# A transformer trunk on one core: loading x feature-major in the first stage and taking its norm sums, and the first scale columns, from single-column matmuls

## The chip, the cores and the metric

The kernel runs on one core of one Trainium2 chip. A core has TensorE (PE in the profile: matmuls, with the weight loads as PEld), VectorE (DVE), ScalarE (ACT), GpSimd (POOL) and SyncE (SP, which here issues nearly all DMA loads). The metric is device microseconds of one execution, the lower the better. The runs shown are medians over three executions.

## The reference, cut to what matters

The network has two layers, 512 tokens of 1024 features, all in float32. Before each mixer and each FFN the input is normed and then scaled and shifted by vectors that come from a condition vector c:

```python
def rms_norm(x, g):
    y = xf * lax.rsqrt(jnp.mean(xf * xf, axis=-1, keepdims=True) + EPS)
    return (y * g.astype(jnp.float32)).astype(x.dtype)

def ada_modulation(c, w, b):
    m = jax.nn.silu(c) @ w + b
    shift, scale, gate = jnp.split(m, 3, axis=-1)

h = rms_norm(x, mix_pre_g[i]) * (1.0 + scale) + shift
qkv = (h @ w_qkv)
```

So the first products need, for each token, one factor (1 over the root of the mean square of its 1024 features) and, for each feature, one scale and one shift, each a sum over 1024 products of silu(c) with a column of the modulation weight. After this first stage come the stick-breaking attention, its output projection, a SwiGLU FFN, a gMLP mixer and a second FFN; the change does not touch them.

## The kernel before

**Operands.** Every float32 product is made from high and low parts: a high part is a copy rounded to the matmul's reduced type (fp32r) by ScalarE, a low part is the difference, by VectorE (`split`, and `wemit` for weights: names wh and wl, made from raw). One product of a tile is three matmuls (`mm3`): high by high, high by low, low by high. The names hTh and hTl are the parts of h, feature-major (features on partitions): eight tiles, here called columns 0 to 7, of 128 features by 512 tokens.

**First stage.** x is loaded token-major in four tiles of 128 tokens by 1024 features. For each, `norm0` squares and sums the rows on ScalarE (accum_out), takes root and reciprocal, and VectorE multiplies the rows by the factor; here the factor is a scalar per partition. `turn0` transposes each tile on TensorE (eight transposes, name tp), and ScalarE or VectorE copies the result out of PSUM into the feature-major tiles xhT.

**Scale columns.** For columns 0 and 1, `row0` makes a row of 256 sums on TensorE (silu(c), name sc, is the stationary column, the weight block of 128x256 moves through; result ab in one partition), VectorE copies the row, and two small matmuls turn it into columns. `scales` adds the biases and multiplies by the norm weights. For columns 2 to 7 the weights are loaded in pairs of columns (blocks of 128x2x512, name ada from ada0p, four blocks for a pair): VectorE sums them in `ada0_sum` (eight operations of 128x512, name acc), and `sums0` closes the sum over the partitions with four single-column matmuls. `h0` makes column k of h: two ScalarE operations with scale and shift (hTh, and the same unrounded, in place) and one VectorE subtraction (hTl).

**Order.** `v_step` and `qk0_step` multiply column k by the weights of v (first half of its features) and of the first pair of heads (pq, pk). The code issues column by column; a loop over three pairs follows columns 0 and 1. Within this stage the order on each engine is chosen by the framework's scheduler from the order in the code and the dependencies, not by hand. From the second half of v on (`pe["chain"] = True` ahead of it) the order of TensorE is the written one, and in the attention VectorE's too. The calls `order` and the flags `chain` of the helper classes at L64 to L99 write such an order.

**Loads.** SyncE issues loads in the order of the code. Weights pass through two buffers named raw (`wload`); a third load waits until VectorE has read the first. The modulation blocks of this stage have eight buffers (tag ra). Loads for columns 2 to 7 stand behind the weight loads in the same queue:

```python
    wqk0.append(wget(("wqk", 0, 1), 0))
    wload()
    acc = ada0_sum(a2, 512, 2)
```

G in the trace is the sum for the gate vector of the first mixer, which VectorE does in the background (`Bg`, bg0).

Of the kernel before, what the change touches and what calls it, by code (L numbers as in the profile page):

```python
# [13 lines left out]
P = 128  # L14
T = 512
# [18 lines left out]
def trunk(ctx: ExitStack, tc: tile.TileContext, A: dict, out: bass.AP):  # L34
# [21 lines left out]
    def slot(dt, name, a=2, b=512):  # L56
        return s4.tile([P, a, b], dt, tag="s4", name=nm(name))
# [302 lines left out]
    x0, a0 = [], []  # L360
    for tt in range(NT):
        xt = slot(F32, "x0", 1, 1024)
        load(xt[:, 0, :], A["x"][tt * P : (tt + 1) * P, :])
        x0.append(xt[:, 0, :])
        if tt == 0:
            identt = consts.tile([P, P], F32, name="identt")
            load(identt[:], A["consts"][:, 0, :])
            cols = consts.tile([P, 4, KD], F32, name="cols")
            load(cols[:], A["cols"])
        elif tt == 3:  # L370
            a0.extend(ada0_raw(0, q) for q in range(2))
    wload()
# [303 lines left out]
    xhT = [slot(F32, "xhT") for _ in range(4)]  # L676

    def norm0(tt):
        xt = x0[tt]
        junk = npool.tile([P, D], F32, tag="n", name=nm("junk"))  # L680
        sx = small.tile([P, 1], F32, tag="sx", name=nm("sx"))
        act.activation(junk[:], xt, AF.Square, accum_out=sx[:])
        sd, r1 = rms(sx[:])
        dve.reciprocal(r1[:], sd[:])
        dve.tensor_scalar(xt, xt, r1[:, 0:1], None, ALU.mult)

    def turn0(tt):
        xt = x0[tt]
        for q in range(2):
            ps = bank("tp0")  # L690
            for k in range(4):
                kk = q * 4 + k
                transpose(ps[:, k * P : (k + 1) * P], xt[:, kk * P : (kk + 1) * P])
            for k2 in range(2):
                dst = xhT[q * 2 + k2][:, :, tt * P : (tt + 1) * P]
                src = ps[:, k2 * 256 : (k2 + 1) * 256].rearrange("p (a b) -> p a b", a=2)
                if q and tt < 2:
                    dve.tensor_copy(dst, src)
                else:
                    act.activation(dst, src, AF.Copy)  # L700
# [37 lines left out]
    onec = oneb[:, 0:1]  # L738

# [24 lines left out]
    def row0(raws):  # L764

        ps = bank("ab0", "p")
        for q, raw in enumerate(raws):
            for k in range(4):
                mm(ps[0:1, :256], sc[:, q * 4 + k : q * 4 + k + 1], raw[:, k, :], q + k == 0, q * 4 + k == 7)
        row = stp.tile([P, 256], F32, tag="row", bufs=2, name=nm("row"))  # L770
        dve.tensor_copy(row[0:1, :], ps[0:1, :256])
        ps = bank("ab0", "p")
        for i in range(2):
            mm(ps[:, i : i + 1], row[0:1, i * P : (i + 1) * P], oneb[0:1, 0:1], True, True)
        return ps

    def scales(ps, k):

        ab = small.tile([P, 2, 2], F32, tag="ab", name=nm("ab"))
        dve.tensor_tensor(ab[:, 0, :], ps[:, :2], add[:, k, :], ALU.add)  # L780
        dve.tensor_tensor(ab[:, 0, :], ab[:, 0, :], mul[:, k, :], ALU.mult)
        return ab

    def h0(ab, i, k):

        xk = xhT[k // 2][:, k % 2, :]
        h, l = hTk(hT, k, 0, T)
        for out in (h, xk):
            act.activation(out, xk, AF.Identity, scale=ab[:, i, 0:1], bias=ab[:, i, 1:2])
        dve.tensor_tensor(l, xk, h.bitcast(F32), ALU.subtract)  # L790
# [8 lines left out]
    norm0(0)  # L799
    norm0(1)  # L800
    turn0(0)
    norm0(2)
    ab0 = row0(a0)
    turn0(1)
    norm0(3)
    turn0(2)
    turn0(3)
# [869 lines left out]
```

## Time and profile before

| What | Value |
|---|---|
| Runs, us | 1104.66, 1107.62, 1107.95; median 1107.62 |
| Profiled execution: span, us | 1104.6 (first to last instruction; the page lists no other time of its own) |
| Instructions | 18512 |
| PE / PEld busy | 98% / 89% |
| DVE / ACT / POOL busy | 86% / 54% / 3% |
| Mean granted TensorE clock | 0.998 |
| HBM read / written | 164.69 MB / 8.39 MB |

Times in the text are microseconds from the first instruction of the profiled execution. A row of a timeline has the start, the duration of the group, the engine, the line, the operation, the tile written, the tiles read, the shapes and the count; in square brackets stands how long the engine was idle before it, and what ended that. A matmul's duration holds its pipeline, so two starts tell more than one duration. A busy share of 98% therefore does not say that TensorE is at its peak.

### The profile page before, as it was taken

The page shows a single profiled execution, that of the slowest core. Times are in us where ns is not written, and L with a number is a line of the kernel's source. Part 1 is how long each engine was busy: PE and PEld are TensorE (multiplying, and loading weights), DVE is VectorE, ACT ScalarE, POOL GpSimd, SP SyncE. Part 2 cuts the span into 40 slices and gives each one's busy share as a digit, 9 for nine tenths or more (in the row PEclk, how much of TensorE's full clock was granted, in tenths as well). Part 3 has the DMA queues.
Part 4 walks back from the last instruction along what each step waited for, and adds up shares of the span by engine and source line. Part 5 has one row for each costly group of instructions (what it writes and reads, how often), then busy time and mean ns, then how long its engine had stood idle before and what let it go on. Part 6 is the DMA issues. An engine that isn't in the chain of part 4 may idle for free.

```text
span 1104.6 us, 18512 instructions
## 1 busy us (share of the span) xinstructions
PE 1085.9 (98%) x7404; PEld 979.0 (89%) x7404; DVE 945.9 (86%) x1248; ACT 594.2 (54%) x982; POOL 29.5 (3%) x53
## 2 busy tenths in 40 slices
PE   6999999999999999999999999999999999999997
PEld 4787788788999999998888889988999999989996
DVE  4988999966989999989866967668979999899997
ACT  6554665665655555554243626426555555565662
POOL 0020100000000000000000000001000000000000
PEclk9999999999999999999999999999999999999999
DMA  8976434304433434359757465334334343333252
GB/s 302 370 226 217 142 116 133 125 11 152 157 112 131 162 119 146 132 197 351 272 191 256 144 205 196 96 116 155 128 117 155 128 159 102 110 115 96 77 187 81
DMA packets 51355, 176.38 MB, mean 160 GB/s; under 512 B 6074, under 2 KB 9146, under 8 KB 51268
## 3 DMA queue, kind: packets, MB, share of 16 engines
q1 hardware_dynamic: 48708, 166.81, 44.6%
q0 software_dynamic: 2560, 8.39, 2.1%
q8 instruction: 58, 0.95, 0.3%
q14 instruction: 29, 0.24, 0.1%
HBM read 164.69 MB, written 8.39 MB: 157 GB/s over the span
## 4 chain that ended last, share of the span: by engine, by line
PE 90%; DVE 4%; DMA 2%; ACT 2%; issue 1%; SPq 0%; DVEq 0%; ACTq 0%
PE r L109 32%; PE y L109 18%; PE pqk L109 7%; PE gu L109 6%; PE v L109 5%; PE X L109 4%; PE u L109 4%; PE Y L109 3%; PE av L109 2%; PE z L109 2%; PE tw L117 1%; PE tp L117 1%; PE Z L109 1%; PE W L109 1%; PE ab L109 1%
## 5 line engine op out<-in xcount | busy, mean ns | idle before, releaser
L87 ACT ACTIVATE wh<-raw 128x1024 fp32r<-128x1024 f32 (+1 forms) x112 | 115.7, 1038 | 130.5 <-PE y L109 39.4
L109 PE MATMUL r<-Sh,wh 128*128 128x256 f32 x608 | 168.1, 276 | 0.5 <-ACT e L87 0.5
L109 PE MATMUL r<-Sh,wl 128*128 128x256 f32 x608 | 167.9, 276 | 0.0
L109 PE MATMUL r<-Sl,wh 128*128 128x256 f32 x608 | 167.9, 276 | 0.0
L109 PE MATMUL y<-wh,as 128*128 128x512 f32 x480 | 149.9, 390 | 0.0
L178 DVE TENSOR_TENSOR wl<-raw,wh 128x1024 fp32r<-128x1024 f32 x87 | 105.8, 1222 | 48.2 <-ACT wh L87 47.6
L109 PEld LDWEIGHTS r<-Sh,wh 128*128 128x128 f32 x608 | 114.1, 188 | 1.0 <-ACT e L87 0.9
L109 PEld LDWEIGHTS r<-Sl,wh 128*128 128x128 f32 x608 | 114.1, 188 | 0.1
L109 PEld LDWEIGHTS r<-Sh,wl 128*128 128x128 f32 x608 | 114.1, 188 | 0.0
L109 PEld LDWEIGHTS y<-wh,as 128*128 128x128 f32 x480 | 90.0, 188 | 18.6
L71 DVE TENSOR_TENSOR wl<-f,wh 128x1024 fp32r<-128x1024 f32 x87 | 103.2, 1220 | 0.0
L87 ACT ACTIVATE wh<-f 128x1024 fp32r<-128x1024 f32 x87 | 91.8, 1055 | 15.3 <-DVE f L71 11.6
L87 ACT ACTIVATE e<-r 128x256 f32<-128x256 f32 x114 | 43.7, 385 | 101.8 <-PE r L109 100.8
L109 PE MATMUL y<-wl,as 128*128 128x512 f32 x240 | 93.7, 391 | 0.0
L109 PE MATMUL r<-hTh,wh 128*128 128x256 f32 x304 | 84.2, 277 | 0.2 <-DVE gu L71 0.2
L109 PE MATMUL r<-hTl,wh 128*128 128x256 f32 x304 | 84.0, 276 | 0.0
L109 PE MATMUL r<-hTh,wl 128*128 128x256 f32 x304 | 84.0, 276 | 0.0
L109 PE MATMUL r<-hTh,b 128*128 128x256 f32 x304 | 57.9, 276 | 0.0
L109 PEld LDWEIGHTS r<-hTh,wh 128*128 128x128 f32 x304 | 57.1, 188 | 0.9 <-DVE gu L71 0.9
L109 PEld LDWEIGHTS r<-hTh,wl 128*128 128x128 f32 x304 | 57.1, 188 | 0.0
L109 PEld LDWEIGHTS r<-hTl,wh 128*128 128x128 f32 x304 | 57.1, 188 | 0.0
L87 ACT ACTIVATE wh<-rawx 128x1024 fp32r<-128x1024 f32 x38 | 40.4, 1063 | 29.8 <-PE r L109 29.0
(262 smaller groups left out, 2937.1 us busy)
## 6 DMA issues: line engine op xcount, KB each, us to landing
rawada<-in_ada SPq DMA_DIRECT2D x80, 512.0 KB, 5.7
rawy<-in_wy SPq DMA_DIRECT2D x38, 512.0 KB, 4.6
rawx<-in_wx SPq DMA_DIRECT2D x38, 512.0 KB, 3.7
raw<-in_wdown SPq DMA_DIRECT2D x22, 512.0 KB, 5.4
raw<-in_wdn SPq DMA_DIRECT2D x22, 512.0 KB, 3.6
raw<-in_wqk SPq DMA_DIRECT2D x16, 512.0 KB, 3.9
ada<-in_ada0p SPq DMA_DIRECT2D x12, 512.0 KB, 6.3
raw<-in_wgu SPq DMA_DIRECT2D x12, 512.0 KB, 3.5
```

The lines of the kernel that those rows point to most:

```text
L71: b = getattr(nc.vector, op)(*args, **kw)
L87: b = nc.scalar.activation(*args, **kw)
L109: b = nc.tensor.matmul(o, l, r, start=start, stop=stop, skip_group_check=True)
L117: last_tp[0] = nc.tensor.transpose(o, i, ident)
L178: last_low[0] = nc.vector.tensor_tensor(l[:], raw[:], h[:].bitcast(F32), ALU.subtract)
```

## The change

The host lays x out feature-major a second time (xT: four tiles of 128 features by 2 by 512 tokens); the first stage reads that one. The first three quarters are loaded whole, the last in two halves; the two blocks for scale column 0 (a0) are loaded after the second and after the fourth quarter, and the first weight (v) in two halves. The other loads keep their order.

The norm sums come from squares: ScalarE squares each quarter (sq), VectorE adds the squares up to one tile of 128x512 and leaves the last half for itself, and TensorE sums over the partitions with single-column matmuls (the squares are the stationary operand, a column of ones moves; result st, one column for 128 tokens). Root and reciprocal are made for all 512 tokens at once. The factors lie across partitions then, so they are spread: VectorE scales the identity by each column of factors (dg), and four matmuls with a stationary tile of ones give rb, the factors of 512 tokens in each partition. `scaled0` multiplies a column of x by rb (columns 0 and 1) or by its copy rs (columns 2 to 7) on VectorE, in place. `h0` is as before, cut in two functions.

For columns 0 and 1, `sums1` takes the place of `row0` and `scales`: the weight block is the stationary operand, a column of sc moves, 16 single-column matmuls for a column, and the biases are put in by a matmul with the identity.

From the first `sums1` to column 1 the order on TensorE, ScalarE and VectorE is written out by the chain flags. In it the first weight's high parts stand ahead of column 0's activations, its low parts around hTl of column 0, and the parts of the first qk weight behind column 1's activations.

```diff
-    for tt in range(NT):
-        xt = slot(F32, "x0", 1, 1024)
-        load(xt[:, 0, :], A["x"][tt * P : (tt + 1) * P, :])
...
+    for j, cuts in enumerate((1, 1, 1, 2)):
+        for i in range(cuts):
+            c = slice(2 * i // cuts, 2 * (i + 1) // cuts)
+            load(xT[j][:, c, :], A["xT"][j][:, c, :])
...
+        elif j == 1:
+            a0.append(ada0_raw(0, 0))
+        elif j == 3:
+            a0.append(ada0_raw(0, 1))
...
+    def squares0():
+
+        for j in range(3):
+            act.activation(sq[j][:], xT[j][:], AF.Square)
+            if j:
+                dve.tensor_tensor(sq[0][:], sq[0][:], sq[j][:], ALU.add)
+        dve.tensor_tensor(sq[0][:, 0, :], sq[0][:, 0, :], sq[0][:, 1, :], ALU.add)
+        for i in range(2):
+            act.activation(sq[3][:, i, :], xT[3][:, i, :], AF.Square)
+        dve.tensor_tensor(sq[0][:, 0, :], sq[0][:, 0, :], sq[3][:, 0, :], ALU.add)
+
+    def stats0():
+
+        mm(st[:, 0:NT], ident, zero[:], True, False)
+        for i, s in enumerate((sq[0][:, 0, :], sq[3][:, 1, :])):
+            for tt in range(NT):
+                mm(
+                    st[:, tt : tt + 1], s[:, tt * P : (tt + 1) * P], onec,
+                    False, i == 1 and tt == NT - 1,
+                )
+        sd = small.tile([P, NT], F32, tag="sd0", bufs=1, name=nm("sd"))
+        last_sqrt[0] = act.activation(sd[:], st[:, 0:NT], AF.Sqrt, bias=epsb[:], scale=1.0 / D)
+        r = small.tile([P, NT], F32, tag="r0", bufs=1, name=nm("r"))
+        dve.reciprocal(r[:], sd[:])
+        for tt in range(NT):
+            dve.tensor_scalar(dg[:, tt, :], ident, r[:, tt : tt + 1], None, ALU.mult)
+            mm(rb[:, tt * P : (tt + 1) * P], onef[:], dg[:, tt, :], True, True)
+
+    def scaled0(k, rb):
+        xk = xT[k // 2][:, k % 2, :]
+        dve.tensor_tensor(xk, xk, rb, ALU.mult)
...
+    def sums1(ps, raw, k, q):
+
+        if q == 0:
+            mm(ps[:, 0:2], ident, add[:, k, :], True, False)
+        for kk in range(4):
+            for i in range(2):
+                mm(
+                    ps[:, i : i + 1], raw[:, kk, i * P : (i + 1) * P],
+                    sc[:, q * 4 + kk : q * 4 + kk + 1], False, q * 8 + kk * 2 + i == 15,
+                )
...
+    pe["chain"] = act.chain = dve.chain = True
+    sums1(pa[0], a0[0], 0, 0)
+    squares0()
+    stats0()
+    for i in range(2):
+        act.activation(wvh[:, i, :], rawv[:, i, :], AF.Copy)
+    ab0 = sums1(pa[0], a0[1], 0, 1)
+    scaled0(0, rb[:])
+    a2 = [ada0_raw(2, q) for q in range(4)]
+    high0(ab0, 0, 0)
+    scaled0(1, rb[:])
+    sums1(pa[1], a1[0], 1, 0)
+    for i in range(2):
+        dve.tensor_tensor(wvl[:, i, :], rawv[:, i, :], wvh[:, i, :].bitcast(F32), ALU.subtract)
+        if i == 0:
+            low0(0)
...
+    act.activation(rs[:], rb[:], AF.Copy)
...
+    ab1 = sums1(pa[1], a1[1], 1, 1)
+    high0(ab1, 0, 1)
+    wqk0.append(wget(("wqk", 0, 0), 0))
+    low0(1)
+    pe["chain"] = act.chain = dve.chain = False
     wqk0.append(wget(("wqk", 0, 1), 0))
     wload()
     acc = ada0_sum(a2, 512, 2)
     for b in range(1, 4):

+        for k in (2 * b, 2 * b + 1):
+            scaled0(k, rs[:])
         ps = cols0(2 * b)
```

104 lines of the change are left out of this document (38 added, 66 removed).

## The prediction

> **What bounds the kernel now.** I read the page's first part, then busy time by stretches, then the timelines of the engines in the first 75 us, because the change ends there.
>
> ```profile
> span 1104.6 us, 18512 instructions
> PE 1085.9 (98%) x7404; PEld 979.0 (89%) x7404; DVE 945.9 (86%) x1248; ACT 594.2 (54%) x982; POOL 29.5 (3%) x53
> ```
>
> TensorE is busy 98% of the span, so time can only come from a stretch in which it does no useful work, and a delay put into a dense stretch stays. The stretches of the first stage (columns: busy us and count of PE, PEld, DVE, ACT, POOL, then granted clock, DMA share, GB/s):
>
> ```profile
> 0.00:7.84 7.84, 0.00 (x1) 0.00 (x1) 1.29 (x9) 4.22 (x6) 1.19 (x6) 1.00 0.67 207
> 7.84:23.72 15.88, 15.04 (x69) 8.18 (x69) 6.58 (x16) 12.18 (x26) 0.00 (x0) 1.00 0.97 398
> 25.16:52.02 26.86, 26.27 (x128) 20.98 (x128) 25.57 (x39) 11.42 (x14) 1.42 (x2) 1.00 0.94 356
> ```
>
> Until 23.72 TensorE transposes x and makes two rows of sums; none of that is a product of the layer. From 25.16 to 52.02 two engines are full at once: PE 26.27 and DVE 25.57 of 26.86 us. The rows of VectorE and ScalarE that frame this stretch:
>
> ```profile
> 21.00 0.85 ACT L87 ACTIVATE hTh<-xhT,ab 128x512 fp32r<-128x512 f32 x1
> 25.16 0.73 DVE L71 SCALAR_TENSOR_TENSOR acc<-ada,sc,acc 128x512 f32<-128x512 f32 x1
> 26.39 0.16 DVE L71 TENSOR_TENSOR ab<-ab,add 128x2 f32<-128x2 f32 x1 [0.51 <-PE ab L109]
> 43.39 0.16 DVE L71 TENSOR_TENSOR ab<-ab,mul 128x4 f32<-128x4 f32 x1
> 46.51 1.29 DVE L71 TENSOR_TENSOR hTl<-xhT,hTh 128x512 fp32r<-128x512 f32 x2
> 52.02 0.16 DVE L71 TENSOR_TENSOR ab<-ab,mul 128x4 f32<-128x4 f32 x1
> 52.21 1.53 ACT L87 ACTIVATE hTh<-xhT,ab 128x512 fp32r<-128x512 f32 x2 [4.74 <-DVE ab L71]
> ```
>
> and of TensorE:
>
> ```profile
> 7.84 1.97 PE L117 MATMUL tp<-identt,x 128*128 128x128 f32 x8 [7.84 <-DVE x L71]
> 12.55 5.12 PE L109 MATMUL ab<-ada,sc 128*1 128x256 f32 x16
> 18.82 1.42 PE L117 MATMUL tp<-identt,x 128*128 128x128 f32 x11
> 20.17 3.61 PE L109 MATMUL ab<-ada,sc 128*1 128x256 f32 x16
> 23.72 0.50 PE L109 MATMUL v<-wh,hTh 128*128 128x512 f32 x1
> 42.41 0.95 PE L109 MATMUL ab<-oneb,acc 128*128 128x1 f32 x8
> 43.22 0.48 PE L109 MATMUL pk<-hTh,wh 128*128 128x512 f32 x1
> 44.46 0.50 PE L109 MATMUL v<-wh,hTh 128*128 128x512 f32 x1 [0.31 <-ACT hTh L87]
> 54.25 0.39 PE L109 MATMUL v<-wh,hTh 128*128 128x512 f32 x1
> ```
>
> Columns 2 to 7 of the layer's input h need scale columns (ab), which VectorE sums up in acc. At 44.46 TensorE waits 0.31 us for hTh of column 4: here VectorE's list sets the pace. For columns 6 and 7 it ends at 52.02; the first of the two hTh is there near 52.98 (52.21 and half of 1.53), and TensorE takes it at 54.25. So VectorE has 1.27 us of cover at the last pair and none at the pair before. This is what decides: a change that lengthens VectorE's list up to the row at 52.02 by more than it starts that list earlier makes TensorE wait.
>
> **The change part by part.** Prices come from groups of rows with their shapes kept apart (count | busy us, mean ns), first 60 us:
>
> ```profile
> L71 DVE SCALAR_TENSOR_TENSOR acc<-ada,sc,acc 128x512 f32<-128x512 f32 x24 | 18.0, 749 | 0.6
> L178 DVE TENSOR_TENSOR wl<-raw,wh 128x1024 fp32r<-128x1024 f32 x7 | 8.5, 1218 | 0.3 <-ACT wh L87 0.3
> L71 DVE TENSOR_TENSOR hTl<-xhT,hTh 128x512 fp32r<-128x512 f32 x8 | 5.2, 684 | 3.2 <-ACT xhT L87 3.2
> L71 DVE TENSOR_SCALAR x<-x,r 128x1024 f32<-128x1024 f32 x4 | 3.0, 754 | 0.1
> L71 DVE RECIPROCAL r<-sd 128x1 f32<-128x1 f32 x4 | 0.6, 160 | 2.0 <-ACT sd L87 1.9
> L87 ACT ACTIVATE junk<-x 128x1024 f32<-128x1024 f32 x4 | 4.2, 1050 | 2.7 <-DMA x<-in_x 2.7
> L87 ACT ACTIVATE vf<-v 128x512 f32<-128x512 f32 x2 | 1.2, 598 | 3.0 <-PE v L109 2.9
> L87 ACT ACTIVATE sd<-sx,epsb 128x1 f32<-128x1 f32 x4 | 1.2, 295 | 0.1
> ```
>
> Loads: SyncE's rows:
>
> ```profile
> 8.12 0.33 SPq L126 DMA_DIRECT2D raw<-in_wqk  x1
> 9.37 0.33 SPq L126 DMA_DIRECT2D ada<-in_ada0p  x1
> 10.64 0.33 SPq L126 DMA_DIRECT2D ada<-in_ada0p  x1
> 11.87 0.33 SPq L126 DMA_DIRECT2D ada<-in_ada0p  x1
> 24.93 0.33 SPq L126 DMA_DIRECT2D raw<-in_wv  x1
> 25.36 2.11 SPq L126 DMA_DIRECT2D ada<-in_ada0p  x4
> ```
>
> Each of the four issues from 8.12 on comes when the load eight places before it has landed (x1, x2, x3, the first scale block), so 512 KB land every 1.25 us. The bytes stay the same and the rate is the limit; only the order moves. A scale block now stands between the second and the third quarter of x, so I put the second quarter at 8.1, the scale block at 9.35, the third at 10.6, the last halves at 11.2 and 11.85, the second scale block at 13.1. The last of x comes 1.25 later than now. The two extra issues (halves) cost nothing while loads stand ahead of them.
>
> Norm: Squares on ScalarE: 1.05 each, halves 0.60 by the vf row, done at 12.9. VectorE adds: two of 1.22 and two of about 0.65, the last done near 14.2. On TensorE a single-column product was there 8 times in the 0.81 us between 42.41 and 43.22, so 0.10 an instruction, two instructions a matmul. The eight matmuls behind the adds take 1.6, to about 16.0. Then square root 0.30, reciprocal 0.16, four scalings of 128x128 (between 0.16 and 0.754; I take 0.2, nearest to the small row), and the last spread matmul (0.25, from 11 transposes in the 1.35 us from 18.82 to 20.17): 17.8. What is removed (32 transposes, their 16 evacuations, four scalings of x by rows at 0.754) lay before 21.0, so none of it shortens VectorE's later list. The copy of the spread factors out of PSUM (0.60) runs on ScalarE behind column 0's activations, while ScalarE waits for the next ab; without that cover the multiplies from column 2 on would start 0.6 later. The memsets of ones and zeros run on engines that wait for the loads.
>
> First scale columns: Sixteen instructions of 0.10 and the product behind them: 19.6. They replace row products of 5.12 and 3.61, which needed a row copy and a turn as well. Then the first multiply by the spread factors, 0.65: hTh starts at 20.4 against 21.00, so 0.6 earlier, and TensorE's first product at 21.2 against 23.72, since the second row (3.61) no longer stands before it.
>
> VectorE until 52.02: With the multiply for column 1, the two low halves of the first weight and hTl of column 0 it is free for acc at about 23.4 against 25.16: -1.75. Into its list come six multiplies of full tiles, for columns 2 to 7. The hTl rows have the same kind and size: 0.684 alone, 1.29 for the two at 46.51, so 3.9 to 4.1; I take +3.9, as they come in pairs. The low half of the first qk weight now comes behind column 1's activations, so it moves into the list: +1.2. Out go the 0.51 us before 26.39, which acc can fill, and one small add: -0.65. Sum -1.75 + 3.9 + 1.2 - 0.65 = +2.7 on the row at 52.02. The cover takes 1.27 of it; TensorE reaches the end of the first products 1.4 us later. ScalarE loses work in the stretch (11.42 of 26.86 busy), which buys nothing.
>
> [...]
>
> What is late next: The second half of v:
>
> ```profile
> 66.39 2.36 DVE L178 TENSOR_TENSOR wl<-raw,wh 128x1024 fp32r<-128x1024 f32 x2 [0.45 <-ACT wh L87]
> 67.85 0.39 PE L109 MATMUL v<-wh,hTh 128*128 128x512 f32 x1
> ```
>
> The first wl is done at 66.39 + 1.18 = 67.57, and TensorE uses it at 67.85: 0.28 of cover. If VectorE carries all of 2.7 that far, TensorE loses 2.4; if its later sums give way, 1.4. I take the middle, +1.9. Against its own execution the sum is 1104.6 + 1.9 = 1106.5. That span is 0.06 under the lowest of the runs (1104.66) and 3.0 under their median (1107.62); I add the step to the median: 1109.5.
>
> **The rivals.** TensorE's head start counts, and VectorE is not the bound: Place: the row that answers 52.02. If the multiplies fall into VectorE's waits, what is left is TensorE starting at 21.2 instead of 23.72 (2.5) and its wait of 0.31 at 44.46: -2.8, so 1104.8. For it: VectorE waits 3.2 us before its hTl rows today, in the first stage. Against it: after 25.16 it has 1.3 us free in all, and acc cannot move ahead of its own loads. It decides if the last ab ends before 52.
>
> VectorE starts its list late: The order of the three engines is written out through column 1; if acc is not put into VectorE's waits for column 1 (about 2 us before ab, 1.7 behind it), its list starts nearer 27.5: +1.9 + 3.7 = +5.6, 1113.2. The same time comes if TensorE runs at half pace through sums and spread: the transposes at 7.84 took 0.25 each and those at 18.82 0.12, though the granted clock reads 1.00 in that stretch. Sums, spread and columns are 1.6 + 1.0 + 1.6 = 4.2 at full pace, so up to +4.2 more. The first scale columns run from 9.4 on, which speaks against it.
>
> [...]
>
> The weight queue holds the sums up: The four loads for the second acc block stand on SyncE behind the next v weight (24.93, then 25.36), and that waits for a buffer which the moved low half frees, now near 30. A load of this kind and the start of that block:
>
> ```profile
> DMA to landing us min/median/max: 5.5/7.1/10.2
> 34.78 1.53 DVE L71 SCALAR_TENSOR_TENSOR acc<-ada,sc,acc 128x512 f32<-128x512 f32 x2
> ```
>
> Issued at 30.4, the first lands at 36 at best, where the forecast has VectorE ready for the block from 34.5 on. Low halves and multiplies can fill the gap, or not: +0 to +2, up to 1111.5.
>
> It comes out level: Later stages give the step back, 1107.6.
>
> **How the numbers follow.** Forecast (+1.4 to +2.4) 0.40; TensorE's head start 0.20; late list 0.14; weight queue 0.12; level 0.14. The likeliest one's own range is 1107.5 to 1111.5 with the spread of the runs. Changes below 0.3% (3.3 us) can't be told from none, as the three runs lie that far apart. Faster by more than that needs all of the head start and a little more: 0.15. Slower needs the late list, or the queue on top of the forecast: 0.27. Within: 0.58. The range goes from a full head start, 1103, to the late list, 1113.5.
>
> **What would show it.** Right: hTh near 20.4, the first v product near 21.2, acc from 23 to 24, the ab row for columns 6 and 7 near 54.5, a wait of TensorE for hTh at column 4 or 6 of 1 to 3 us, VectorE without gaps between. Wrong: that ab row at 52 or before (then the head start counts); acc from 27 (late list); single-column instructions at 0.2 before 20 us (slow array); VectorE waiting for ada loads near 35 (queue). If hTh starts after 21.0, the working of the norm is wrong, whatever the total.

## The result, and the profile after

The changed kernel takes 1147.12 us (median of four runs, 1144.32 to 1147.99), the kernel before 1106.61 beside it (1104.66 to 1107.95): a ratio of 1.0362, 95% interval 1.0341 to 1.0383. The forecast was 1109.5, its range ended at 1113.5. The sign was the forecast's; of the 40.5 us it had 1.9.

The page of the kernel after, its first rows (busy us, share of the span, instructions):

```profile
span 1145.4 us, 18541 instructions
PE 1122.2 (98%) x7426; PEld 1013.5 (88%) x7426; DVE 948.7 (83%) x1251; ACT 591.4 (52%) x966; POOL 29.7 (3%) x54
```

TensorE is busy 36.3 us longer (1122.2 against 1085.9) with 22 instructions more. So most of the time doesn't go into waits: the same products take longer. Where, is read from the start of the first or last instruction of some products (views by tile; us):

| Product | before | after | later by |
|---|---|---|---|
| first v product | 23.7 | 28.4 | 4.7 |
| first z product (attention) | 73.4 | 90.9 | 17.5 |
| first r product (gMLP weights) | 315.1 | 334.3 | 19.2 |
| first u product | 632.4 | 661.0 | 28.6 |
| first X product | 981.2 | 1020.7 | 39.5 |
| last store | 1101.0 | 1141.9 | 40.9 |

Two losses, then: 17.5 us until z, in the stage that was changed, and 23.4 us behind it, in code that the change does not touch; 20.3 of these grow between the first r and the first X product.

**The first stage.** TensorE's timeline of the kernel after:

```profile
9.47 3.54 PE L109 MATMUL ab<-sc,ada 128*128 128x1 f32 x16 [3.04 <-DMA ada<-in_ada0s]
14.51 3.57 PE L109 MATMUL st<-oneb,sq 128*128 128x1 f32 x16 [1.07 <-DVE sq L71]
19.06 2.04 PE L109 MATMUL rb<-dg,onef 128*128 128x128 f32 x8 [0.98 <-DVE dg L71]
20.90 3.41 PE L109 MATMUL ab<-sc,ada 128*128 128x1 f32 x16
24.60 3.55 PE L109 MATMUL ab<-sc,ada 128*128 128x1 f32 x16
28.44 2.05 PE L109 MATMUL v<-wh,hTh 128*128 128x512 f32 x4
30.29 1.91 PE L109 MATMUL v<-wl,hTh 128*128 128x512 f32 x4
32.00 1.91 PE L109 MATMUL v<-wh,hTl 128*128 128x512 f32 x4
33.70 2.21 PE L109 MATMUL ab<-sc,ada 128*128 128x1 f32 x16
38.17 0.63 PE L109 MATMUL v<-wh,hTh 128*128 128x512 f32 x1
```

Sixteen single-column instructions take 3.4 to 3.6 us, 0.22 each, four times in a row; the prediction had 0.10, from a row at 42.41. The twelve v products from 28.44 to 33.70 come every 0.44 us where the kernel before has 0.23. The array works at half pace from the first instruction (two bias instructions at 5.84 take 0.58 us, the same kind 0.28 at 27.32 in the kernel before) to about 35 us; there the fifth group of sixteen needs only 2.21. At 38.17 it is at half pace again (starts 0.43 apart until 40.73). VectorE of the kernel after:

```profile
18.63 0.87 DVE L71 TENSOR_SCALAR dg<-identt,r 128x128 f32<-128x128 f32 x4
28.64 0.75 DVE L71 SCALAR_TENSOR_TENSOR acc<-ada,sc,acc 128x512 f32<-128x512 f32 x1
35.95 0.16 DVE L71 TENSOR_TENSOR ab<-ab,mul 128x2 f32<-128x2 f32 x1 [6.57 <-PE ab L109]
47.23 0.16 DVE L71 TENSOR_TENSOR ab<-ab,mul 128x4 f32<-128x4 f32 x1
67.14 0.16 DVE L71 TENSOR_TENSOR ab<-ab,mul 128x4 f32<-128x4 f32 x1 [1.72 <-PE ab L109]
```

It begins its list at 28.64 with one operation and then stands 6.57 us: the second column's factors come next in its order, and TensorE has them late. The row that answers 52.02, the factors of columns 6 and 7, comes at 67.14. Stretches from 36 us on (columns as in the prediction), kernel after:

```profile
36.00:40.00 4.00, 3.37 (x11) 2.67 (x12) 4.00 (x7) 3.52 (x4) 0.00 (x0) 0.74 0.00 0
44.00:48.00 4.00, 2.63 (x14) 1.94 (x14) 3.99 (x8) 1.63 (x2) 0.75 (x2) 1.00 0.98 355
48.00:52.00 4.00, 3.71 (x10) 2.94 (x11) 3.96 (x8) 3.31 (x5) 0.67 (x1) 0.57 1.02 413
60.00:64.00 4.00, 3.70 (x12) 2.92 (x13) 3.89 (x7) 4.00 (x7) 0.00 (x0) 0.72 0.34 136
```

In two places the granted clock falls in the stretch behind one in which TensorE stood (idle 1.37 of 4 us at 44, clock 0.57 at 48; idle 0.80 of 4 us at 56, clock 0.72 at 60). In the kernel before, all these stretches show 1.00. The account from the first v to the first z product, one stretch of each kernel, before first:

```profile
23.72:73.40 49.68, 49.09 (x229) 39.58 (x228) 45.45 (x57) 22.70 (x30) 9.56 (x18) 1.00 0.84 302
```

```profile
28.44:90.90 62.46, 58.45 (x237) 46.56 (x237) 46.21 (x61) 24.56 (x32) 9.58 (x18) 0.92 0.70 251
```

The stretch is 12.8 us longer. TensorE is idle 4.0 against 0.6 us: 3.4. Granted clock, 58.45 at 0.92: 4.7. Half pace from 28.44 to 35, which the granted clock doesn't show (it reads 1.00 there): 5.3 us for twelve products instead of 2.8, and 0.3 in the sums behind them: 2.8. That leaves 1.9, of which the dearer single product (next) is about 1.2 (237 at 5 ns). With the 4.7 of the later start this is the 17.5.

**The later stages.** Groups with their shapes kept apart (count | busy us, mean ns), before and after:

```profile
L109 PE MATMUL r<-Sh,wh 128*128 128x256 f32 x608 | 168.1, 276 | 0.5 <-ACT e L87 0.5
L109 PE MATMUL y<-wh,as 128*128 128x512 f32 x480 | 149.9, 390 | 0.0
```

```profile
L109 PE MATMUL r<-Sh,wh 128*128 128x256 f32 x608 | 171.1, 281 | 0.0
L109 PE MATMUL y<-wh,as 128*128 128x512 f32 x480 | 152.1, 395 | 0.0
```

Same counts, same shapes, no waits, and each product 5 ns dearer. Nothing in these rows says why; that is what the first experiments ask.

### The profile page after: what moved, and what is told of

It is laid out like the page before. It is cut to its first block, busy times and chain, and to the rows that moved or that the text cites. A ratio compares the mean times of both kernels' runs of the same rounds, so it can differ in the third digit from the quotient of the medians.

```text
span 1145.4 us, 18541 instructions
## 1 busy us (share of the span) xinstructions
PE 1122.2 (98%) x7426; PEld 1013.5 (88%) x7426; DVE 948.7 (83%) x1251; ACT 591.4 (52%) x966; POOL 29.7 (3%) x54
## 4 chain that ended last, share of the span: by engine, by line
PE 96%; DVE 2%; ACT 1%; DMA 1%; issue 0%; SPq 0%; DVEq 0%; ACTq 0%
PE r L109 33%; PE y L109 18%; PE v L109 8%; PE pqk L109 7%; PE gu L109 6%; PE X L109 4%; PE u L109 4%; PE Y L109 3%; PE av L109 2%; PE z L109 2%; PE tw L117 1%; PE Z L109 1%; PE W L109 1%; PE tp L117 1%; PE ab L109 1%; DMA xT<-in_xT 1%
## 5 line engine op out<-in xcount | busy, mean ns | idle before, releaser
L87 ACT ACTIVATE wh<-raw 128x1024 fp32r<-128x1024 f32 (+2 forms) x113 | 115.7, 1030 | 142.8 <-PE y L109 48.1
L109 PE MATMUL r<-Sh,wh 128*128 128x256 f32 x608 | 171.1, 281 | 0.0
L109 PE MATMUL r<-Sh,wl 128*128 128x256 f32 x608 | 170.7, 281 | 0.0
L109 PE MATMUL r<-Sl,wh 128*128 128x256 f32 x608 | 170.6, 281 | 0.0
```

The lines of the kernel that those rows point to most:

```text
L87: b = nc.scalar.activation(*args, **kw)
L109: b = nc.tensor.matmul(o, l, r, start=start, stop=stop, skip_group_check=True)
```

## The experiments

Eighteen kernels. Ratios are against the kernel before on the same chip (its medians there were 1105.77 to 1106.49).

| Run | Median us | Ratio, 95% interval |
|---|---|---|
| after, addresses as before (e1) | 1124.74 | 1.0175 [1.0156, 1.0194] |
| before, with the three tiles (e2) | 1129.99 | 1.0225 [1.0210, 1.0241] |
| before, slots moved by 64 bytes (e3) | 1128.39 | 1.0209 [1.0189, 1.0229] |
| before, all moved by 32 (e4) | 1105.81 | 1.0003 [0.9991, 1.0016] |
| before, slots by 128 (e12) | 1112.19 | 1.0059 [1.0043, 1.0076] |
| before, slots by 32 (e17) | 1126.80 | 1.0183 [1.0167, 1.0200] |
| before, slots by 192 (e18) | 1128.06 | 1.0191 [1.0176, 1.0206] |
| e1, array kept busy (e5) | 1124.73 | 1.0169 [1.0137, 1.0201] |
| e1, norm part alone (e6) | 1120.30 | 1.0130 [1.0114, 1.0145] |
| before, columns part alone (e7) | 1120.07 | 1.0131 [1.0112, 1.0149] |
| before, array kept busy (e8) | 1104.78 | 0.9990 [0.9981, 1.0000] |
| e5, acc into the wait (e9) | 1122.70 | 1.0146 [1.0130, 1.0162] |
| e5, no six multiplies (e10) | 1117.58 | 1.0103 [1.0088, 1.0118] |
| e5, busy in the wait (e11) | 1125.73 | 1.0174 [1.0149, 1.0199] |
| e1, busy between sums (e13) | 1120.35 | 1.0131 [1.0114, 1.0148] |
| e13, acc into the wait (e14) | 1117.91 | 1.0110 [1.0095, 1.0125] |
| e14, no six multiplies (e15) | 1118.79 | 1.0113 [1.0098, 1.0128] |
| e6, array kept busy (e16) | 1120.37 | 1.0122 [1.0107, 1.0138] |

### The later stages: three small tiles

The change adds three tiles of four floats per partition: `zero` in the pool of constants, `sd0` and `r0` in the pool of small tiles. As the author read the compiled kernel's memory plan, each takes 32 bytes per partition, the constants lie ahead of the weight tiles, and the small tiles between the weight tiles and the slots of the activations. So the weight tiles begin 32 bytes later and the slots 96 (the plan itself is not shown here; the expectations of e1 to e4 go by these figures). One run takes the displacement out of the change, three put it into the kernel before.

e1, the change with its three tiles in the first stage's own pool:

```diff
-    zero = consts.tile([P, NT], F32, name="zero")
+    zero = stp.tile([P, NT], F32, name="zero")
...
-        sd = small.tile([P, NT], F32, tag="sd0", bufs=1, name=nm("sd"))
+        sd = stp.tile([P, NT], F32, name=nm("sd"))
...
-        r = small.tile([P, NT], F32, tag="r0", bufs=1, name=nm("r"))
+        r = stp.tile([P, NT], F32, name=nm("r"))
```

> The changed kernel with its three small new tiles (zero, sd, r of the norm) moved from the long-lived pools to the pool of the first stage, so that all later tiles lie at the addresses that they have in the kernel before (in the changed kernel the weight tiles wh and wl lie 32 bytes higher, the activation slots and the FFN's work tiles 96 bytes higher). Nothing else differs. Theory addresses: the part of the loss behind the first stage (40.8 less the 17.5 by which the first z product is late, so 23) goes, time near 1124, r matmuls at 276 ns mean instead of 281, first z product still near 91. Rival (another order of instructions or the slower start carried on): 1146, r matmuls stay at 281 ns.

e2, the kernel before with three tiles that nothing reads; e3 has only the loop, e4 only `zero`:

```diff
+    zero = consts.tile([P, NT], F32, name="zero")
+    dve.memset(zero[:], 0.0)
+    for t in ("sd0", "r0"):
+        dve.memset(small.tile([P, NT], F32, tag=t, bufs=1, name=nm(t))[:], 0.0)
```

> The kernel before with three tiles of 16 bytes per partition added that nothing reads, in the pools where the change adds its own: weight tiles +32 bytes, activation slots and FFN tiles +96, as in the changed kernel. Theory addresses: 1106.6 + 23 = 1130, first z product unmoved near 73.4, r matmuls 281 ns. Rival: 1106.6.

> The kernel before with only two of these tiles: weight tiles at their old addresses, activation slots and all that follows +64 bytes. If the distance between the stationary and the moving operand counts (64 bytes changed, as in the changed kernel): 1130. If the place of the weights alone counts: 1106.6. If three small tiles never mattered: 1106.6.

> The kernel before with only the third tile: weights, slots and all that follows together +32 bytes, distances kept. If the distance between operands counts: 1106.6. If the place of the weights itself counts: 1130.

Measured: with the addresses kept 22.4 us of the change's 40.5 are gone (1124.74), and its products cost what they cost before:

```profile
L109 PE MATMUL r<-Sh,wh 128*128 128x256 f32 x608 | 168.2, 277 | 1.0 <-ACT e L87 1.0
L109 PE MATMUL y<-wh,as 128*128 128x512 f32 x480 | 150.0, 390 | 0.0
```

The kernel before with three unread tiles loses about as much (+24.2). Its first z product comes at 73.0 and its last store at 1123.8, 1050.8 us apart; in the changed kernel it is 1051.0, in the kernel before 1027.6. The groups of e3, in which only the slots moved:

```profile
L109 PE MATMUL r<-Sh,wh 128*128 128x256 f32 x608 | 171.1, 281 | 0.0
L109 PE MATMUL y<-wh,as 128*128 128x512 f32 x480 | 152.1, 395 | 0.0
```

and e4, in which weights and slots moved together, has the time of the kernel before (1105.81 against 1105.82). e17, below, has its slots at the same place as e4 and its weights 32 bytes lower, and is slow (1126.80). What follows for these kernels: the 23 us come from the distance between the weight tiles and the slots, that is between the two operands of a product, not from the place of either and not from the new instructions.

Three more distances, with the same loop over four, one and six names:

```diff
+    for t in ("sd0", "r0", "sd1", "r1"):
+        dve.memset(small.tile([P, NT], F32, tag=t, bufs=1, name=nm(t))[:], 0.0)
```

> The kernel before with four unread small tiles instead of two: the activation slots move by 128 bytes against the weight tiles, which stay. If what cost 21 us at a distance changed by 64 bytes is the distance in a pattern that repeats every 128 bytes (57,408 bytes before, which leaves 64; 57,472 there, which leaves 0): no change, 1106 us, the products of the middle stage (r) at 276 ns. If any growth of the distance, or the place of the slots against something else, costs: 1128 us or more and 281 ns.

> The kernel before with one unread small tile: the activation slots move by 32 bytes against the weight tiles, which stay (distance 57,440 bytes; by 256 it leaves 96, where 64 was fast for all products, 128 slow for all, 192 slow for those of 512 columns alone, y and v). If the slowness begins at 128: no change, 1106 us, r 276 and y 390 ns. If it depends on whether the distance is a multiple of 64 alone: some other value of both.

> The kernel before with six unread small tiles: the activation slots move by 192 bytes against the weight tiles (distance 57,600 bytes; by 256 it leaves 0). If the pattern repeats every 256 bytes and 0 is as good as 64: 1106 us, r 276 and y 390 ns. If 0 is as bad as 128: 1128 us, r 281 and y 395. If it does not repeat by 256, the larger distance may be slow for either group alone: about 1112 (y, v alone) or 1122 (r, gu alone).

The groups of e12 (slots moved by 128):

```profile
L109 PE MATMUL r<-Sh,wh 128*128 128x256 f32 x608 | 168.1, 276 | 0.3 <-ACT e L87 0.3
L109 PE MATMUL y<-wh,as 128*128 128x512 f32 x480 | 152.1, 395 | 0.0
```

of e17 (by 32):

```profile
L109 PE MATMUL r<-Sh,wh 128*128 128x256 f32 x608 | 170.5, 280 | 0.0
L109 PE MATMUL y<-wh,as 128*128 128x512 f32 x480 | 152.3, 395 | 0.0
```

and of e18 (by 192):

```profile
L109 PE MATMUL r<-Sh,wh 128*128 128x256 f32 x608 | 170.9, 281 | 0.0
L109 PE MATMUL y<-wh,as 128*128 128x512 f32 x480 | 151.5, 394 | 0.0
```

Of five distances only that of the kernel before is fast for both kinds of product; at 128 the r products are fast and the y products slow, and the time lies between (+6.3). A pattern that repeats every 128 bytes is out, since e12 should then have been level. For the r products the fast distances are not one range either: moved by 0 and 128 they are fast (276 ns), by 32 and 64 between them slow (280 and 281). Which rule the distances follow stays open.

### The first stage: half pace, or waits

With the addresses kept, the first z product of e1 still comes at 88.0 (expected near 91) instead of 73.4. Two runs take the change apart (e6 the norm, e7 the single-column sums of the scale columns), two keep the array busy with products that are thrown away (e5 in e1, e8 in the kernel before). There is one profile of each run. Seven kernels with the first stage of the kernel before (before, e2 to e4, e12, e17, e18) have their first v product between 22.1 and 24.2 and their first z product between 72.0 and 74.3; a difference of less than 2 us in either therefore says little. From the first v to the first z product these seven agree within 0.8 us (49.6 to 50.4).

e5:

```diff
+    def warm(n):
+        for _ in range(n):
+            mm(vb[3][:], onef[:], wt[:], True, True)
...
+    warm(5)
     sums1(pa[0], a0[0], 0, 0)
+    warm(3)
     squares0()
...
+    warm(1)
     sums1(pa[1], a1[0], 1, 0)
```

with one more behind the norm's sums.

> The changed kernel with addresses kept, and ten more products of 512 columns whose result is thrown away (a tile of ones by a tile of ones, into a PSUM bank that v uses later): five before the first column sums, three behind them, one while the root is taken, one before the second column's sums. They add work and take none away. Theory clock: TensorE runs at half pace in the changed kernel until 35 us because single-column matmuls do not open its clock, so these ten give full pace: sums of the squares 1.7 us instead of 3.57, column sums 1.7 instead of 3.4, the first hTh near 19.8 instead of 24.2, the first z product near 78 instead of 88.0, time 1124.7 - 10 = 1114. What is then left over the kernel before (8) is VectorE's longer list and the order. Rival (half pace is not the cause, VectorE's list and the waits are): 1124.7 + 1 for the added work, z at 88 or later.

e6, rows as before for the first two scale columns, `rowpart` and `rowend` being the two halves of `row0` and `scales`:

```diff
-    sums1(pa[0], a0[0], 0, 0)
+    rowpart(pa[0], a0[0], 0)
...
-    ab0 = sums1(pa[0], a0[1], 0, 1)
+    rowpart(pa[0], a0[1], 1)
+    ab0 = rowend(pa[0], 0)
```

> One part of the change undone: the first two scale columns by row products of 256 columns as in the kernel before, in the written order; the norm by single-column sums stays, addresses kept. Theory clock: the row products open the clock as they did before (12.55 to 15.77), so the stage gets most of the ten us back: z near 80, time 1116. Rival (the norm part with its written order and VectorE's list makes the loss): z near 88, 1124.

e7, in the kernel before:

```diff
-    ab0 = row0(a0)
+    pa = [bank("ab0", "p") for _ in range(2)]
+    sums1(pa[0], a0[0], 0, 0)
+    ab0 = sums1(pa[0], a0[1], 0, 1)
...
-    ab1 = row0(a1)
+    sums1(pa[1], a1[0], 1, 0)
+    ab1 = sums1(pa[1], a1[1], 1, 1)
```

> The kernel before with only its first two scale columns by single-column matmuls (addresses kept, order left to the scheduler). Theory clock: without the row products nothing opens the clock ahead of v, single columns take 0.22 each and the first dozen v products 0.43, z 3 to 5 us late, time 1110. Rival (single columns are simply cheaper): 2 us of TensorE work saved ahead of v, 1104.

e8, in the kernel before:

```diff
+    warm(5)
...
+    warm(1, last_tp[0])
     norm0(2)
+    turn0(1)
+    warm(1, last_tp[0])
     ab0 = row0(a0)
-    turn0(1)
```

(so the second turn now stands ahead of the first row of sums as well).

> The kernel before with seven such thrown-away products: five before the first transposes, one behind each of the first two transposed tiles. Theory clock: transposes and the first row of sums run at full pace (5.12 becomes 3.6), which stands on the path to the first hTh at 21.0: first v product 1.5 to 2 earlier, time 1104. Rival (the loads of x set that path, not the pace): 1105.8.

TensorE's timeline of e5:

```profile
15.51 1.93 PE L109 MATMUL st<-oneb,sq 128*128 128x1 f32 x16
22.11 1.93 PE L109 MATMUL ab<-sc,ada 128*128 128x1 f32 x16
24.12 1.17 PE L109 MATMUL v<-wh,hTh 128*128 128x512 f32 x4
26.95 1.84 PE L109 MATMUL ab<-sc,ada 128*128 128x1 f32 x16
29.89 0.79 PE L109 MATMUL v<-wh,hTh 128*128 128x512 f32 x1 [0.36 <-ACT hTh L87]
30.48 0.63 PE L109 MATMUL v<-wl,hTh 128*128 128x512 f32 x1
```

The same sixteen instructions take 1.93 us behind dense products and 3.57 without: that the half pace is made by what stands ahead of them, and not by their form, is shown. But at 29.89, behind sixteen of them and some 1.1 us with little else, the products are at half pace again (starts 0.43 apart from 30.48 to 34.32, granted clock 0.50 from 32 to 36). First z 82.5 instead of 88.0, last store 1115.3 instead of 1120.2 in the profiles; the median doesn't move, and the four runs lie 8 us apart (1120.57 to 1128.84). The profile is of the fastest of the four, so its 82.5 flatters e5, and how much of e1's loss the half pace makes isn't settled by it.

In e7 the sums of one column stand at half pace even between transposes:

```profile
12.03 3.55 PE L109 MATMUL ab<-sc,ada 128*128 128x1 f32 x16 [0.28 <-DMA ada<-in_ada0s]
17.39 3.41 PE L109 MATMUL ab<-sc,ada 128*128 128x1 f32 x16
22.48 3.55 PE L109 MATMUL ab<-sc,ada 128*128 128x1 f32 x16
27.74 3.41 PE L109 MATMUL ab<-sc,ada 128*128 128x1 f32 x16
```

First v at 25.9, first z at 84.7: 58.9 us between them, 9 more than before. e7 is the cleanest test of the half pace: VectorE has none of the six multiplies and the order is the scheduler's, as before, and still the loss comes. It was to be 3 to 5 us at z, and is 11.4. Rows of e7, VectorE's first, then the stretches behind TensorE's wait of 2.25 us for acc at 41.23:

```profile
31.19 0.16 DVE L71 TENSOR_TENSOR ab<-ab,mul 128x2 f32<-128x2 f32 x1 [4.88 <-PE ab L109]
34.92 6.26 DVE L71 SCALAR_TENSOR_TENSOR acc<-ada,sc,acc 128x512 f32<-128x512 f32 x8
```

```profile
40.00:44.00 4.00, 2.77 (x11) 2.58 (x12) 3.30 (x5) 0.83 (x2) 1.00 (x2) 0.68 0.85 299
44.00:48.00 4.00, 4.00 (x10) 3.10 (x10) 3.93 (x7) 2.93 (x4) 0.41 (x1) 0.50 0.97 367
```

VectorE waits for the slow sums and its list for columns 2 and 3 starts at 34.92 instead of 25.16; TensorE then waits for the list, and is at half pace behind the wait. In e6 the sums of the norm are at full pace (1.95 for sixteen at 14.58) behind eight row products of 256 columns, but eight rows take 3.57 twice; first z at 86.6, between what the theory (80) and the rival (88) had said. Each half of the change costs 14 us alone, and the whole with the addresses kept 19, so the two costs don't add. No run has the change in the scheduler's order; what the written order costs by itself is not shown. In e8 the first row of sums takes 3.61 instead of 5.12 and the first v product comes at 21.8; the median is 1.0 us under the kernel before, at the edge of its interval. No other version is under it.

e5 left two readings for the rest. V: VectorE's list sets the end (its later start and the six multiplies). C: half pace behind TensorE's waits sets it. Three runs on top of e5. e9, half of the sum of columns 2 and 3 written ahead of VectorE's wait:

```diff
+    for i in range(4):
+        ada_stt(acc[:], a2[i // 2][:, i % 2, :], i)
     ab1 = sums1(pa[1], a1[1], 1, 1)
...
-    acc = ada0_sum(a2, 512, 2)
+    for i in range(4, 8):
+        ada_stt(acc[:], a2[i // 2][:, i % 2, :], i)
```

> The run with the array kept busy, and the first four of the eight acc operations of columns 2 and 3 written ahead of the wait in which VectorE stood 2.65 us for the second column's sums (28.83 us there). Everything is still computed. Theory V, VectorE's list sets the end of the first stage: the list starts 2.65 us sooner and never stands; the scale factors of columns 2 and 3, at 41.26 us there, come at 38.6, the first z product goes from 82.5 to about 80, although the second column's own factors come some 2 us later (about 31) and TensorE stands longer before them. Theory C, TensorE's half pace after each of its waits (30 to 36 us and 43 to 46 there) sets it: a longer wait of TensorE near 30 us leaves the clock closed at least as long, and the first z product stays at 82.5 or comes later.

e10:

```diff
-        for k in (2 * b, 2 * b + 1):
-            scaled0(k, rs[:])
```

> The run with the array kept busy, without the six multiplies of columns 2 to 7 by the row factors (those columns go unnormalised, so this part of the computation is left out). Theory V (VectorE's list): two of the six ran inside a wait, four (2.7 us) stood in the list; factors of columns 2 and 3 at 39 instead of 41.26, and by the last columns 3 to 4 us sooner (60.7 to 57), first z product near 79. Theory C (half pace): TensorE still waits for the second column near 29 us and loses its clock for 6 us; first z product 81.5 to 82.5.

e11:

```diff
     ab1 = sums1(pa[1], a1[1], 1, 1)
+    hold(pa[1], 6)
```

where `hold` is six thrown-away products of 256 columns.

> The run with the array kept busy, with six more thrown-away products of 256 columns behind the second column's sums, where TensorE stood 1.1 us and then worked at half pace from 29.9 to 36 us. Theory V (VectorE's list): the products behind them go at 0.23 instead of 0.43 and end some 3 us sooner, TensorE then waits that much longer for acc, the factors of columns 2 and 3 stay at 41.2 and the first z product at 82.5 (within 0.7). Theory C (half pace): the 3 us are kept, first z product at 79.5 or sooner.

First z products: 85.1, 82.7 and 83.1, against 82.5 in e5. None is sooner, so the numbers forecast for z by V (e9, e10) and by C (e11) all fell. But the runs do not decide between V and C, because half pace set in at another place in each (near 18 us in e9, 22 in e10, 23 in e11, 29 in e5), although TensorE's instructions are the same up to there: first v products at 29.1, 25.8 and 23.4, against 24.1. From the first v to the first z product it is 56.0, 56.9 and 59.7 us, against 58.4, so behind the first v product V's two edits do save 2.3 and 1.5. (The median of e9 is 2.0 under e5's, within e5's spread. That of e10 is 7.1 under it, and its slowest run, 1117.85, is faster than e5's fastest; in the two profiles the gain comes behind z.) TensorE in e9:

```profile
18.27 1.78 PE L109 MATMUL rb<-dg,onef 128*128 128x128 f32 x8
19.84 3.41 PE L109 MATMUL ab<-sc,ada 128*128 128x1 f32 x16
```

and in e10:

```profile
19.45 1.84 PE L109 MATMUL ab<-sc,ada 128*128 128x1 f32 x16
22.23 3.31 PE L109 MATMUL ab<-sc,ada 128*128 128x1 f32 x16
```

The same single columns (at 19.84 and 19.45) are at half pace in one run and at full pace in the other. Hence three runs with short products between the sums, each on top of the one before. Some of their thrown-away products stand in the PSUM bank of the sums of columns 2 and 3, behind the matmul that puts the biases in, so the scale factors of these two columns are not those of the network (by the code they lose the biases; no view shows values). The trace has 36 thrown-away products in e13, not 31 as its expectation says: ten ahead of the first sums, four behind their first half, the rest between and behind. e13 (`warm` is now one product of 256 columns):

```diff
                     sc[:, q * 4 + kk : q * 4 + kk + 1], False, q * 8 + kk * 2 + i == 15,
                 )
+            if kk == 1:
+                warm(1)
+        if q == 0:
+            warm(1)
...
     ab1 = sums1(pa[1], a1[1], 1, 1)
+    warm(4)
...
+        if k == 2:
+            warm(5)
         for i in range(4):
             mm(ps[:, i : i + 1], acc[:, i * P : (i + 1) * P], onec, False, i == 3)
+        if k == 2:
+            warm(2)
```

> The run with the addresses kept, with 31 thrown-away products of 256 columns written between the single-column sums (after every fourth of them, during the root, and during TensorE's waits near 30 and near 40 us): the run with bursts between whole sums closed the clock again between 19 and 29 us, at another place in each run. Theory B (the lost time of the first stage, 14.6 us by the first z product, is TensorE's half pace in two places, and what is left with the clock open is VectorE's list): single columns at 0.11 to 0.12 all through, first v product near 24 to 25 us, the v and pq products of columns 0 and 1 at 0.23, and with VectorE's list as the bound factors of columns 2 and 3 at 41, the next ones 9.8 and 18.5 us later as before, first z product near 80.5. Theory S (the bursts themselves and the written order cost what they save): first z product at 83 or later although the clock stays open.

e14 has the edit of e9 on top, e15 that of e10 as well.

> The run before this one, with the first four acc operations of columns 2 and 3 written ahead of VectorE's wait for the second column's sums. With the clock open VectorE's list is the bound (theory B): its stand of some 2.6 us goes, first z product 2 to 2.6 us sooner than in that run, near 78. If TensorE's work and waits bound it (theory S): no gain, as in the run that did this without an open clock (85.1).

> The run before this one, without the six multiplies of columns 2 to 7 (those columns go unnormalised, so this part of the computation is left out). Theory B: VectorE's list is shorter by up to 3.9 us, first z product 2.5 to 3.9 us sooner, near 75, that is within 2 us of the kernel before (73.4); the whole within 0.3% to 0.5% of it. Theory S: less than 1 us.

First z products: 85.7, 84.0, 83.6. The stretches of e15:

```profile
24.00:28.00 4.00, 4.00 (x21) 3.77 (x21) 3.44 (x6) 1.95 (x3) 0.00 (x0) 0.65 0.11 8
28.00:32.00 4.00, 4.00 (x11) 3.03 (x11) 1.78 (x3) 0.00 (x0) 0.00 (x0) 0.50 0.94 357
36.00:40.00 4.00, 4.00 (x19) 3.35 (x18) 3.96 (x6) 2.52 (x3) 0.00 (x0) 1.00 0.06 7
30.70:83.60 52.90, 52.90 (x255) 44.46 (x253) 43.89 (x55) 24.91 (x33) 9.56 (x18) 0.99 0.79 283
```

Half pace set in once more, between 23 and 26 us, in all three (the granted clock from 24 to 28 us is 0.50, 0.66 and 0.65): one short product behind every eight single-column instructions didn't prevent it. From 32 us on the granted clock is 0.99 to 1.00 until z. There TensorE stands 2.65 us in all in e13, 2.4 of it for acc and for the hTh that come behind it, 0.30 in e14 and not at all in e15 (52.90 of 52.90 us busy in the last row). So at full pace VectorE's list did cost TensorE 2.4 us, and e9's edit takes that away: from the first v to the first z product 59.8, 56.6 and 56.1 us. The six multiplies then cost 0.4 at z (e14 against e15), too little to tell from nothing. Theory B fell in its numbers (80.5, 78 and 75 were its z products). Theory S has the z products of e13 and e15, but its condition, a clock open throughout (full pace), was not met, and e14's 1.7 at z is nearer to B's 2 to 2.6 than to S's nothing. What keeps e15 behind the kernel before is its first v product, 3.8 later (27.5), the twelve products behind it at half pace (4.9 us instead of 2.8) and its thrown-away products, of which those behind the first v product take 4.9 us.

e16 asks the same of the norm part alone (e6 with `warm(10)` ahead, 4, 3 and 6 behind).

> The run of the norm part alone (first two scale columns by products along rows, as before; addresses kept), with 23 thrown-away products of 256 columns: ten ahead, four behind the first row of sums, three behind the norm's sums, six around the turn of the second row. In that run the rows were at half pace twice (3.57 us for eight instructions) and the clock closed at 32 to 36 and 44 to 52 us. Theory B (half pace is what the norm part costs): rows at 1.9, first v product at 23.5 to 24 instead of 26.1, the stretch of 32 to 36 us at full clock, first z product at 80 to 82 instead of 86.6. Theory S (its written order and its waits cost it): first v product sooner, first z product still at 85 or later.

The stretch from 32 to 36 us has a granted clock of 1.00 now (0.69 in e6), as theory B said; first z comes at 85.8, against 86.6, as theory S said, and the median is e6's. The first v product comes at 26.8, against 26.1, where both had it sooner. TensorE stands 1.5 us for hTl, 1.6 for hTh and 1.1 for the squares, and half pace is back from 15.7 to 21.6 and in part from 44 to 52 (0.75 and 0.82; 0.50 and 0.67 in e6). So neither theory is shown for the norm part; how much of its time is waits and how much is pace stays open.

Behind z, e1 loses 4.6 us more (1032.2 from z to the last store against 1027.6). In the attention TensorE waits 2.7 us for accl in e1, and behind that wait the granted clock is 0.83 from 110 to 120 us; the two make some 4.4 us. The wait is 1.2 in e6 and 0.8 in e10, which lose only 1.1 there and show a clock of 1.00 behind it. The kernel before and the changed kernel have no such wait. What moves it wasn't tried.

## Why the prediction was wrong, point by point

**The price of a single-column instruction: the term that failed.** The step said "a single-column product was there 8 times in the 0.81 us between 42.41 and 43.22, so 0.10 an instruction". The row is read rightly, but it is of a stretch at full pace; the instructions that it had to price stand ahead of any dense product. They took 0.22. Down the chain of the prediction: sums done 18.1 (forecast 16.0), spread done 20.9 (17.8), first columns 24.3 (19.6), hTh 25.13 (20.4), first v product 28.44 (21.2). The other terms of that chain were close: the adds were done at 14.5 (14.2), the first block of scale weights was there at 9.47 (9.35), the root took 0.26 (0.30), the four scalings 0.87 (0.8). (The terms written for 17.8 add up to 17.5; that slip is small beside the rest.)

**The rival that had it, at 0.14, was priced once.** It named half pace "through sums and spread" with "up to +4.2 more", from the transposes at 0.25. The last sentence, "The first scale columns run from 9.4 on, which speaks against it", took it that these columns would bring the array to full pace. They didn't: in the kernel after TensorE does nothing from 9.47 to 28.44 but single columns, short bias matmuls and the eight instructions of the spread, and is still at half pace then (v products 0.44 us apart), and in e7 single columns and transposes (0.22 and 0.25 us each) are at half pace from 7.7 to 25.9. The rival also counted neither the second column's sums (3.55 in the row at 24.60), nor the first v products behind them, nor that half pace comes back later: in the kernel after TensorE was idle from 33.9 to 37.0 us for 0.25 and 0.46 us only, with sixteen single columns and the two instructions for the next biases in the rest, and from 38.2 to 40.7 the products came every 0.43 us. What brings half pace back there is not shown.

**The late list.** The other half of that rival, acc not put into the wait, happened: 6.57 us at 35.95, where the prediction had put 2 and 1.7. The sign named for it (acc from 27) and that of the slow array (0.2 before 20 us) both showed.

**VectorE as the bound.** Sizes were right: 0.68 a multiply (forecast 0.65), the low half moved in at 1.22 (1.2). The step that failed is the sum "-1.75 + 3.9 + 1.2 - 0.65 = +2.7 on the row at 52.02": it takes TensorE at full pace for granted. The row came 15.1 later (67.14), VectorE waiting for TensorE 1.56 and 1.72 us at the last two pairs. TensorE's waits that the forecast had did come (1.10 us for hTh at 60.30), but all of TensorE's idle time from v to z is only 3.4 us more than before. With the granted clock at 0.99 to 1.00 from 32 us on, VectorE's list cost TensorE 2.4 us until acc was put into the wait, and the six multiplies then 0.4, not 3.9 (e13 to e15). So the right sign is in the main luck: the delay that it was forecast from is a small part of the 40.5.

**The later stages.** The sum was made for the first 70 us, and only one rival let later stages move at all, to give time back. More than half of the loss lies there: 23.4 us, and three unread tiles in the kernel before make 23.2 of the same kind. This term was put at nothing, and no step looked at where the new tiles lie. The diff shows the new tiles; what a distance costs the profile of before could not show, as it has one distance only.

**The queue.** VectorE waited for no modulation block of columns 2 to 7; that rival didn't come.

**The range.** The two bounds that the prediction had, +3.7 and +4.2, stood side by side as alternatives. Both came. But even added to the forecast's 1.9 they give 9.8, against 17.5 at z, and the 23 us of the later stages came on top.

## What to carry to other kernels

Take a price only from a row at the same array pace: here sixteen single-column instructions took 1.93 us behind dense products (e5) and 3.4 to 3.6 in a stage made of them, and the twelve v products behind that stage took 5.3 us instead of 2.8. Before a change is judged, compare the memory plans: here three small tiles in pools ahead of the big ones cost 22.4 of the change's 40.5 us (e1), and three unread tiles of that size in the old kernel showed it in one run (e2, +24.2). When two engines are both full, test the removal of two causes together as well as one by one. And compare stretches between the same two instructions, not only the time at which one comes, when the start itself moves from run to run.

## What the runs showed of the hardware that was not expected

In these kernels the distance between the operands of a product decided some 5 ns of each: 276 against 281 ns for r, 390 against 395 for y, over a whole kernel 20 to 24 us (2%). Weights and slots moved together by 32 bytes cost nothing (e4, 1105.81 against 1105.82 us); the slots alone moved by 32, 64 or 192 made both kinds slow (280 to 281 and 394 to 395 ns), by 128 only y of the two (276 and 395).

The granted clock of the profile read 1.00 while single-column instructions took 0.22 and products came every 0.44 us (stretches before 36 us of the kernel after), so in this stage the distance of starts showed the pace and the granted clock did not. Where half pace set in behind the sums of the norm varied: near 18, 22, 23 and 29 us in four kernels (e9, e10, e11, e5) whose TensorE has the same instructions up to there.
